# A dilated convolution on one core: two more input pairs loaded unconverted on SyncE's queue and converted by ScalarE

## The chip, the cores and the metric

The kernel runs on one core of a Trainium2 chip. The metric is the device time of one execution in microseconds (us). One execution of the kernel before was also recorded by the hardware profiler; all durations of single instructions come from that one. The engines go by the profile's names: PE (TensorE), DVE (VectorE), ACT (ScalarE), POOL (GpSimd) and SP (SyncE). All their transfers run on the core's 16 DMA engines.

## The reference

A 3x3 convolution with dilation 2 and zero padding 2, over 16 images of 64 channels, to 128 channels, in f32:

```python
batch, c_in, h, w, c_out, k, dilation = 16, 64, 64, 64, 128, 3, 2
...
x_pad = np.pad(x, ((0, 0), (0, 0), (pad, pad), (pad, pad)), mode='constant')
for b, co, ci, kh, kw in ...:
    output[b, co] += weight[co, ci, kh, kw] * x_pad[b, ci, kh*2:kh*2+h, kw*2:kw*2+w]
```

## The kernel before, in words

Two images make a pair: their 2 x 64 channels fill the 128 partitions, and each partition holds one channel's 64 x 64 values. There are eight pairs, 2 MB each in f32. Each pair's output is 4 MB in f32, two images of 128 channels.

Rows that lie two apart meet in the dilated kernel, so the kernel combines them: for each group of four rows it forms the sum of the two halves once (`s16`, by `prepare` on GpSimd, L140) and multiplies that sum by the middle row of weights; the remaining terms use differences of weights (`w21`, `w01`) and the outer rows (`w0`, `w2`), on the f16 values `x16`. The weights are turned once at the start (L98 to L127).

A pair is worked in four steps `u` of 16 rows. A step has three phases of matmuls (`phase`, L185), each for both images: the first, on `s16`, is copied by ScalarE to `s32` (L202); the other two, on `x16`, are added to `s32` by VectorE and written to the output buffer `o` (L207). SyncE stores `o` (L218): the first and the last pair in two halves, the others whole, one DMA an image.

The input gets in by two ways. Pair 0 is loaded in f32 on SyncE's queue, in two pieces, right behind the weights (L74), into one half of a buffer that otherwise holds outputs; VectorE and ScalarE convert it (L129, L131), and `prepare(0)` reads the f32 values. Pairs 1 to 7 are loaded on GpSimd's queue, which converts f32 to f16 on the way (`load`, L80). Load 1 is issued between GpSimd's two weight subtractions (L109), loads 2 to 4 after the first piece of `prepare(0)` (L146), and loads 5 to 7 from inside the loop, two pairs ahead (L194).

The order on each engine is that of the program (`manual_schedule`), and waits come from the tiles' dependencies. Buffers: six for `x16`, three for `s16`, two for `s32`, three output buffers of 4 MB (`opool`), four pairs of banks for matmul results.

Of the kernel before, what the change touches and what calls it, by code (L numbers as in the profile page):

```python
# [10 lines left out]
def kernel(  # L11
# [7 lines left out]
    nc = tc.nc  # L19

    B, CI, H, W = x.shape
# [5 lines left out]
    P = 128  # L27
    f32 = mybir.dt.float32
    f16 = mybir.dt.float16
# [20 lines left out]
    x16pool = ctx.enter_context(tc.tile_pool(name="x16pool", bufs=6))  # L50
    sumpool = ctx.enter_context(tc.tile_pool(name="sumpool", bufs=3))
    spool = ctx.enter_context(tc.tile_pool(name="spool", bufs=2))
    opool = ctx.enter_context(tc.tile_pool(name="opool", bufs=3))
# [5 lines left out]
    x_pair = x.rearrange("(nb two) c h w -> nb (two c) h w", two=2)  # L59
# [5 lines left out]
    x16 = {}  # L65
# [2 lines left out]


    cuts0 = [0, 20, 36, 52, H]  # L70
    x32 = opool.tile([P, 2, H, W], f32, tag="o", name="x32")[:, 0]
    x16[0] = x16pool.tile([P, H, W], f16, tag="x16", name="x16_0")
    for lo, hi in ((0, 36), (36, H)):
        nc.sync.dma_start(out=x32[:, lo:hi], in_=x_pair[0, :, lo:hi])  # L74


    def load(pb, cuts):
        x16[pb] = x16pool.tile([P, H, W], f16, tag="x16", name=f"x16_{pb}")
        for lo, hi in zip(cuts, cuts[1:]):
            nc.gpsimd.dma_start(out=x16[pb][:, lo:hi], in_=x_pair[pb, :, lo:hi])  # L80

    AHEAD = 5
# [16 lines left out]
    for name, a in (("w21", 2), ("w01", 0)):  # L99
        for u in range(2):  # L100
            eng = nc.vector if name == "w21" else nc.gpsimd
            eng.tensor_sub(  # L102
                out=w16[:, SLOT[name] * KW : (SLOT[name] + 1) * KW, u, :],
                in0=w32k[:, a * KW : (a + 1) * KW, :],
                in1=w32k[:, KW : 2 * KW, :],
            )

            if name == "w01" and u == 0:
                load(1, [0, H])  # L109

    w_sb = wpool.tile([P, NS * KW, CO], f16, name="w_sb")
    for n, name in enumerate(("w1", "w21", "w0", "w01", "w2")):
        ps = cpool.tile([P, 2, NB], f32, tag="ps", name=f"wt{n}")
        k0 = SLOT[name] * KW
        for j in range(KW):
            nc.tensor.matmul(  # L116
                out=ps[:, 0, j * CO : (j + 1) * CO],
                lhsT=w16[:, k0 + j, :, :].rearrange("o t i -> o (t i)"),
                rhs=ident,
                start=True,  # L120
                stop=True,
            )
        dst = w_sb[:, k0 : k0 + KW, :].rearrange("p k o -> p (k o)")
        if n % 2 == 0:
            nc.vector.tensor_copy(out=dst, in_=ps[:, 0, 0 : KW * CO])  # L125
        else:
            nc.scalar.copy(out=dst, in_=ps[:, 0, 0 : KW * CO])  # L127
        if n == 0:
            nc.vector.tensor_copy(out=x16[0][:, 0:20], in_=x32[:, 0:20])  # L129
    for lo, hi in zip(cuts0[1:], cuts0[2:]):  # L130
        nc.scalar.copy(out=x16[0][:, lo:hi], in_=x32[:, lo:hi])  # L131


    def prepare(pb, lo, hi):
        if pb not in s16:
            s16[pb] = sumpool.tile([P, 2 * NQ, W], f16, tag="s16", name=f"s16_{pb}")
        src = (x16[pb] if pb else x32).rearrange("p (q e r) w -> p q e (r w)", e=2, r=2)
        dst = s16[pb].rearrange("p (q r) w -> p q (r w)", r=2)
        q0, q1 = lo // 4, hi // 4
        nc.gpsimd.tensor_add(  # L140
            out=dst[:, q0:q1], in0=src[:, q0:q1, 0, :], in1=src[:, q0:q1, 1, :]
        )

    prepare(0, 0, 20)
    for pb in range(2, AHEAD):
        load(pb, [0, H])  # L146
    for lo, hi in zip(cuts0[1:], cuts0[2:]):
        prepare(0, lo, hi)

    def conv(pb, hb, ps, u, terms):  # L150

        p0 = hb * CI
        po = ps.rearrange("p (h w) -> p h w", w=W)
        n, total = 0, len(terms) * KW
        for name, e, shift in terms:
            for kw in KWS:
                dw = (kw - 1) * d
                lo = max(u * UR, -2 * shift)
                hi = min((u + 1) * UR, 2 * NQ - 2 * shift)
                cl, ch = max(0, -dw), min(W, W - dw)  # L160
                q0, q1 = (lo + 2 * shift) // 2, (hi + 2 * shift) // 2
                if e == 2:
                    rhs = s16[pb][p0 : p0 + CI, 2 * q0 : 2 * q1, cl + dw : ch + dw]
                else:
                    rhs = x16[pb].rearrange("p (q e r) w -> p q e r w", e=2, r=2)[
                        p0 : p0 + CI, q0:q1, e, :, cl + dw : ch + dw
                    ]
                o_ap = po[:, lo - u * UR : hi - u * UR, cl:ch]
                if e != 2:
                    o_ap = o_ap.rearrange("p (q r) w -> p q r w", r=2)  # L170
                yield dict(
                    out=o_ap,
                    lhsT=w_sb[p0 : p0 + CI, SLOT[name] * KW + kw, :],
                    rhs=rhs,
                    start=(n == 0),
                    stop=(n == total - 1),
                )
                n += 1

    def phase(pb, u, terms):  # L180

        ps = cpool.tile([CO, 2, NB], f32, tag="ps", name="ps")
        for pair in zip(*(conv(pb, hb, ps[:, hb], u, terms) for hb in range(2))):
            for m in pair:
                nc.tensor.matmul(**m)  # L185
        return ps

    for pb in range(NP):
        o = opool.tile([P, 2, H, W], f32, tag="o", name=f"o{pb}")
        ov = o.rearrange("p b (q e r) w -> p b q e (r w)", e=2, r=2)  # L190
        for u in range(NU):

            if u == 1 and AHEAD <= pb + 2 < NP:
                load(pb + 2, [0, H])  # L194
            if pb + 1 < NP:
                if u == 1:
                    prepare(pb + 1, 0, 36)
                elif u == 2:
                    prepare(pb + 1, 36, H)

            s32 = spool.tile([P, 2, NB], f32, tag="s32", name="s32")
            nc.scalar.copy(out=s32, in_=phase(pb, u, [("w1", 2, 0)]))  # L202
            for e, terms in enumerate(
                ([("w21", 1, 0), ("w0", 1, -1)], [("w01", 0, 0), ("w2", 0, 1)])
            ):
                ps = phase(pb, u, terms)
                nc.vector.tensor_add(  # L207
                    out=ov[:, :, u * UQ : (u + 1) * UQ, e, :],
                    in0=ps.rearrange("p b (q c) -> p b q c", c=QW),
                    in1=s32.rearrange("p b (q c) -> p b q c", c=QW),  # L210
                )


            step = NU // 2 if pb in (0, NP - 1) else NU
            if (u + 1) % step == 0:
                fl = slice((u + 1 - step) * 4 * UQ, (u + 1) * 4 * UQ)
                for hb in range(2):
                    nc.sync.dma_start(out=out[2 * pb + hb, :, fl], in_=o[:, hb, fl])  # L218
# [35 lines left out]
```

## Time and profile before

| | us |
|---|---|
| median of 3 runs | 127.03 |
| lowest and highest | 126.87, 127.39 |
| the profiled execution, its own time | 126.65 |
| its span | 124.9 |
| PE busy | 105.8 |
| VectorE busy | 80.8 |
| GpSimd busy | 41.5 |
| ScalarE busy | 39.6 |

The span is the time from the first to the last record of the profile; the execution's own time is 1.75 us longer. The granted TensorE clock was at 0.9 or more of full speed in every slice in which PE worked through. The page divides the span into 40 slices of 3.12 us; a digit is the busy share of a slice in tenths. A converting load is counted in the profile by the f16 bytes that it writes, 1 MB a pair, and reads twice that.

| DMA | count | KB each | median us from issue to landing |
|---|---|---|---|
| weights, SP | 1 | 288 | 2.8 |
| pair 0, SP | 2 | 1152 and 896 | 5.8 and 8.1 |
| pairs 1 to 7, POOL, converting | 7 | 1024 | 14.6 |
| stores, SP | 12 and 8 | 2048 and 1024 | 17.1 and 12.4 |

### The profile page before, as it was taken

The page shows a single profiled execution, that of the slowest core. Times are in us where ns is not written, and L with a number is a line of the kernel's source. Part 1 is how long each engine was busy: PE and PEld are TensorE (multiplying, and loading weights), DVE is VectorE, ACT ScalarE, POOL GpSimd, SP SyncE. Part 2 cuts the span into 40 slices and gives each one's busy share as a digit, 9 for nine tenths or more (in the row PEclk, how much of TensorE's full clock was granted, in tenths as well). Part 3 has the DMA queues.
Part 4 walks back from the last instruction along what each step waited for, and adds up shares of the span by engine and source line. Part 5 has one row for each costly group of instructions (what it writes and reads, how often), then busy time and mean ns, then how long its engine had stood idle before and what let it go on. Part 6 is the DMA issues. An engine that isn't in the chain of part 4 may idle for free.

```text
span 124.9 us, 2260 instructions
## 1 busy us (share of the span) xinstructions
PE 105.8 (85%) x981; PEld 56.6 (45%) x981; DVE 80.8 (65%) x71; ACT 39.6 (32%) x40; POOL 41.5 (33%) x33
## 2 busy tenths in 40 slices
PE   6359999999999999999999999999999999940000
PEld 2044555555555555555554555555555655510000
DVE  0470777787777777777739977777777777770000
ACT  4768123333333333333332333333332433300000
POOL 2879989395193019302910191000000000000000
PEclk9999999999999999999999999999999999999555
DMA  4999999999999999999999999999999999999990
GB/s 142 355 356 215 215 215 205 262 286 270 396 278 273 360 297 320 409 365 318 297 375 433 441 425 430 430 420 420 420 441 446 417 430 420 430 415 423 423 396 39
DMA packets 4329, 43.42 MB, mean 348 GB/s; under 512 B 480, under 2 KB 480, under 8 KB 736
## 3 DMA queue, kind: packets, MB, share of 16 engines
q1 hardware_dynamic: 3312, 35.95, 68.8%
q0 software_dynamic: 1008, 7.34, 28.5%
q8 instruction: 7, 0.11, 0.3%
q14 instruction: 2, 0.02, 0.0%
HBM read 17.07 MB, written 33.55 MB: 405 GB/s over the span
## 4 chain that ended last, share of the span: by engine, by line
PE 79%; DMA 5%; DVE 2%; POOL 2%; DVEq 1%; issue 0%; SPq 0%
PE ps L185 79%; DMA x<-in_x_dram 5%; DVE o L207 2%; POOL s L140 2%; DVEq L249 1%; SPq L63 0%; DVEq L207 0%
## 5 line engine op out<-in xcount | busy, mean ns | idle before, releaser
L207 DVE TENSOR_TENSOR o<-ps,s 128x1024 f32<-128x1024 f32 x64 | 76.8, 1223 | 26.4 <-PE ps L185 24.6
L185 PE MATMUL ps<-x,w_sb 64*128 64x496 f16 (+3 forms) x768 | 85.9, 369 | 0.1
L185 PEld LDWEIGHTS <-w_sb 64*128 64x128 f16 x960 | 54.3, 95 | 48.4 <-issue 3.7
L202 ACT COPY s<-ps 128x1024 f32<-128x1024 f32 x32 | 32.4, 1012 | 65.5 <-PE ps L185 65.5
L140 POOL TENSOR_TENSOR s<-x 128x1152 f16<-128x1152 f16 (+4 forms) x18 | 35.1, 1975 | 31.1 <-PE ps L185 27.7
L185 PE MATMUL ps<-s,w_sb 64*128 64x496 f16 (+1 forms) x192 | 26.6, 379 | 1.5 <-POOL s L140 1.5
L80 POOL DMA_DIRECT2D x<-in_x_dram x7 | 4.0, 579 | 0.0
L92 PE MATMUL warm<-zero 128*128 128x512 f16 x6 | 2.7, 630 | 1.2 <-DVE zero L86 1.2
L116 PE MATMUL wt<-ident,w 128*128 128x128 f16 x15 | 1.8, 312 | 2.0 <-ACT w L98 2.0
L102 DVE TENSOR_TENSOR w<-w 128x192 f16<-128x192 f32 x2 | 1.5, 799 | 2.4 <-DMA w<-in_weight_dram 2.4
L131 ACT CAST x<-x 128x1024 f16<-128x1024 f32 (+1 forms) x3 | 2.8, 974 | 0.8 <-DMA x<-in_x_dram 0.8
L116 PEld LDWEIGHTS <-w 128*128 128x128 f16 x15 | 1.5, 145 | 3.0 <-ACT w L98 3.0
L98 ACT CAST w<-w 128x576 f16<-128x576 f32 x2 | 2.3, 1220 | 1.6 <-DMA w<-in_weight_dram 1.6
L102 POOL TENSOR_TENSOR w<-w 128x192 f16<-128x192 f32 x2 | 1.9, 952 | 2.3 <-DMA w<-in_weight_dram 2.3
L125 DVE CAST w_sb<-wt 128x384 f16<-128x384 f32 x3 | 1.6, 553 | 1.4 <-PE wt L116 1.4
L92 PEld LDWEIGHTS <-zero 128*128 128x128 f16 x6 | 0.7, 137 | 2.3 <-DVE zero L86 1.2
L98 ACT ACT_TABLE_LOAD x1 | 1.3, 1283 | 0.7 <-PEq L235 0.7
L127 ACT CAST w_sb<-wt 128x384 f16<-128x384 f32 x2 | 1.0, 478 | 1.1 <-PE wt L116 1.1
L86 DVE MEMSET zero<- 128x256 uint32 x1 | 0.3, 272 | 0.9 <-PEq L235 0.9
L129 DVE CAST x<-x 128x1280 f16<-128x1280 f32 x1 | 0.8, 817 | 0.0
masks.py:199 POOL TENSOR_SCALAR_AFFINE_SELECT ident<-ident 128x128 f16<-128x128 f16 x1 | 0.3, 292 | 0.1
masks.py:197 POOL MEMSET ident<- 128x128 f16 x1 | 0.2, 204 | 0.3 <-POOLq L235 0.3
(4 smaller groups left out, 0.4 us busy)
## 6 DMA issues: line engine op xcount, KB each, us to landing
out_dram<-o SPq DMA_DIRECT2D x12, 2048.0 KB, 17.1
out_dram<-o SPq DMA_DIRECT2D x8, 1024.0 KB, 12.4
x<-in_x_dram POOLq DMA_DIRECT2D x7, 1024.0 KB, 14.6
x<-in_x_dram SPq DMA_DIRECT2D x1, 1152.0 KB, 5.8
x<-in_x_dram SPq DMA_DIRECT2D x1, 896.0 KB, 8.1
w<-in_weight_dram SPq DMA_DIRECT2D x1, 288.0 KB, 2.8
```

The costliest lines, as they stand in the source:

```text
L80: nc.gpsimd.dma_start(out=x16[pb][:, lo:hi], in_=x_pair[pb, :, lo:hi])
L92: nc.tensor.matmul(out=warm[:, 0], lhsT=zero[:, 0:P], rhs=zero, start=True, stop=True)
L98: nc.scalar.copy(out=w16[:, 0:NK, u, :], in_=w32k)
L102: eng.tensor_sub(out=w16[:, SLOT[name] * KW : (SLOT[name] + 1) * KW, u, :], in0=w32k[:, a * KW : (a + 1) * KW, :], in1=w32k[:, KW : 2 * KW ...
L116: nc.tensor.matmul(out=ps[:, 0, j * CO : (j + 1) * CO], lhsT=w16[:, k0 + j, :, :].rearrange("o t i -> o (t i)"), rhs=ident, start=True, st ...
L125: nc.vector.tensor_copy(out=dst, in_=ps[:, 0, 0 : KW * CO])
L131: nc.scalar.copy(out=x16[0][:, lo:hi], in_=x32[:, lo:hi])
L140: nc.gpsimd.tensor_add(out=dst[:, q0:q1], in0=src[:, q0:q1, 0, :], in1=src[:, q0:q1, 1, :])
L185: nc.tensor.matmul(**m)
L202: nc.scalar.copy(out=s32, in_=phase(pb, u, [("w1", 2, 0)]))
L207: nc.vector.tensor_add(out=ov[:, :, u * UQ : (u + 1) * UQ, e, :], in0=ps.rearrange("p b (q c) -> p b q c", c=QW), in1=s32.rearrange("p b ( ...
L249: with _tile.TileContext(nc) as tc:
```

## The change

Pairs 1 and 2 are now loaded like pair 0: in f32, on SyncE's queue, each as one DMA, issued right behind pair 0's two pieces. Pair 1 takes the other half of the output buffer that pair 0 stands in, pair 2 half of the next one. So output 0 takes the third buffer, output 1 the first, output 2 the second. ScalarE converts each of the two pairs in three pieces (rows 0 to 16, 16 to 32, 32 to 64), one behind its copy to `s32` in steps 1, 2 and 3 of the pair before. `prepare` reads the f32 values for pairs 0 to 2. GpSimd's load 1 and load 2 are gone; its loads 3 and 4 are issued after the whole of `prepare(0)`. Loads 5 to 7 stay where they are. No matmul, add or store changes.

```diff
-    x32 = opool.tile([P, 2, H, W], f32, tag="o", name="x32")[:, 0]
-    x16[0] = x16pool.tile([P, H, W], f16, tag="x16", name="x16_0")
-    for lo, hi in ((0, 36), (36, H)):
-        nc.sync.dma_start(out=x32[:, lo:hi], in_=x_pair[0, :, lo:hi])
+    PLAIN = 3
+    x32 = []
+    for pb in range(PLAIN):
+        if pb % 2 == 0:
+            stage = opool.tile([P, 2, H, W], f32, tag="o", name=f"x32_{pb}")
+        x32.append(stage[:, pb % 2])
+        x16[pb] = x16pool.tile([P, H, W], f16, tag="x16", name=f"x16_{pb}")
+        for lo, hi in ((0, 36), (36, H)) if pb == 0 else ((0, H),):
+            nc.sync.dma_start(out=x32[pb][:, lo:hi], in_=x_pair[pb, :, lo:hi])
+
+    def cast(eng, pb, lo, hi):
+        eng(out=x16[pb][:, lo:hi], in_=x32[pb][:, lo:hi])
...
-            if name == "w01" and u == 0:
-                load(1, [0, H])
...
-        src = (x16[pb] if pb else x32).rearrange("p (q e r) w -> p q e (r w)", e=2, r=2)
+        src = (x32[pb] if pb < PLAIN else x16[pb]).rearrange("p (q e r) w -> p q e (r w)", e=2, r=2)
...
     prepare(0, 0, 20)
-    for pb in range(2, AHEAD):
-        load(pb, [0, H])
     for lo, hi in zip(cuts0[1:], cuts0[2:]):
         prepare(0, lo, hi)
+
+    for pb in range(PLAIN, AHEAD):
+        load(pb, [0, H])
...
             nc.scalar.copy(out=s32, in_=phase(pb, u, [("w1", 2, 0)]))
+            if pb + 1 < PLAIN and u:
+                lo, hi = ((0, 16), (16, 32), (32, H))[u - 1]
+                cast(nc.scalar.copy, pb + 1, lo, hi)
```

More of the change, by code (lines that the diff above doesn't have):

```diff
@@ L128 @@
         if n == 0:
-            nc.vector.tensor_copy(out=x16[0][:, 0:20], in_=x32[:, 0:20])
+            cast(nc.vector.tensor_copy, 0, 0, 20)
     for lo, hi in zip(cuts0[1:], cuts0[2:]):
-        nc.scalar.copy(out=x16[0][:, lo:hi], in_=x32[:, lo:hi])
+        cast(nc.scalar.copy, 0, lo, hi)
     def prepare(pb, lo, hi):
```

## The prediction

> **What bounds the kernel now.** I read the page first, for the share of busy time along the span; then the windows, for the transfer rate stage by stage; then the chain of waits; then the waits of each engine.
>
> ```profile
> PE   6359999999999999999999999999999999940000
> DMA  4999999999999999999999999999999999999990
> q1 hardware_dynamic: 3312, 35.95, 68.8%
> q0 software_dynamic: 1008, 7.34, 28.5%
> ```
>
> PE works without a break from slice 3 and stops in slice 35. The 16 DMA engines are full from slice 1 to slice 38, four slices longer. The queues' shares add up to 97.3% of the span: SyncE's queue (q1) moved the weights, pair 0 and all stores, GpSimd's (q0) the seven converting loads. Those count 7.34 MB as written in f16, and read twice that in f32.
>
> ```profile
> 109.61 1.23 DVE o L207
> 110.83 1.13 DVEq L249
> ```
>
> The chain of waits ends in the last add, at 110.84 us. The 14 us after it belong to no compute engine. What runs there is seen in the windows (columns: window, length, busy us of each engine, granted clock, DMA share, GB/s):
>
> ```profile
> 0.00:2.00 2.00, 0.81 (x2) 0.28 (x3) 0.27 (x1) 1.26 (x1) 0.70 (x6) 1.00 0.15 21
> 2.00:3.50 1.50, 1.50 (x5) 0.45 (x3) 0.00 (x0) 0.02 (x1) 0.00 (x0) 1.00 1.03 335
> 3.50:5.00 1.50, 0.43 (x2) 0.00 (x0) 1.41 (x2) 1.42 (x2) 1.36 (x2) 1.00 0.99 350
> 5.00:8.00 3.00, 1.78 (x15) 1.61 (x16) 1.58 (x4) 1.93 (x4) 2.20 (x3) 1.00 0.98 408
> 9.00:18.00 9.00, 8.75 (x66) 4.32 (x67) 4.05 (x4) 3.70 (x4) 9.00 (x9) 1.00 1.03 215
> 21.00:22.50 1.50, 1.50 (x18) 0.79 (x16) 0.99 (x1) 1.01 (x1) 1.50 (x2) 1.00 1.07 169
> 80.00:110.00 30.00, 30.00 (x294) 16.52 (x292) 23.05 (x20) 10.12 (x10) 0.00 (x0) 1.00 1.01 427
> 110.00:120.00 10.00, 0.61 (x8) 0.18 (x4) 1.96 (x2) 0.00 (x0) 0.00 (x0) 0.78 1.00 425
> ```
>
> After PE stops, stores drain at 425 GB/s, the rate they had beside PE (427). From 9 to 18 us only converting loads move: 215 GB/s written is 430 GB/s read. Counted by the f32 side, every stage after 5 us is thus near 410 to 430 GB/s with a DMA share near 1.0, whatever the mix. The end is set by the sum of transfers, 50.6 MB (16.8 of x, 0.3 of weights, 33.55 of output), begun at about 2 us. 50.6 / 0.427 = 118.5 us; the slow windows before 5 us, the dip at 21 us and the end of the last store account for the rest of the 124.9.
>
> ```profile
> SPq L218 <- DVE o L207: 100.1, 10, 16.8
> POOL s L140 <- PE ps L185: 27.7, 4, 8.4
> ACT s L202 <- PE ps L185: 65.5, 31, 2.6
> ```
>
> SyncE waits for results and never for room, and GpSimd and ScalarE wait mostly for PE: the compute engines have slack, and DMA has none.
>
> **How much slack.** The last four stores (1 MB each) need 4.2 MB / 0.427 = 9.8 us, the last two 4.9 us. Those two are issued from 112.0 us. The queue is still full to about 123.5 us, so their data need come to the front only at 118.6; allowing 2 to 3 us for a DMA to start, PE may be 3 to 4 us late before the end moves.
>
> **The change, part by part.**
>
> *Bytes.* Pairs 1 and 2 are read in f32 in both kernels. On the f32 side nothing is added or removed.
>
> *Rate of the two loads.* This is the only term on the path. Converting: 4.194 MB / 0.430 = 9.75 us for the two. A plain 2 MB load alone in steady state is not in the trace, so I bound it. By the queues' shares: q0 took 0.285 x 124.9 / 7 = 5.09 us a load; q1 took 0.688 x 124.9 = 85.9 us for 35.95 MB, or 5.01 us for 2.097 MB; two loads gain 0.15 us. By the stores' windows (427 GB/s): 9.82 us, 0.07 us lost. By pair 0's own load, the only plain load of x: 350 and 408 GB/s in 3.5 to 8 us, mean 389, so 10.78 us, 1.03 us lost; by its later part alone (408), 0.53 us lost. I take 0.0, between the first two, because stores have the same queue and the same 16 KB per partition as the new loads, while pair 0 runs in the start-up, where the rate still climbs from 335. Both ends, -0.15 and +1.03, stay for the range.
>
> *Order at the start.* Today GpSimd issues load 1 at 4.69 us, loads 2 to 4 from 9.14. Afterwards SyncE issues pairs 1 and 2 right behind pair 0, at about 2.1 to 2.9 us (two issues of 0.42 us each). The engines were full from 2 us anyway, so starting earlier fills no hole: 0 us. Before 2 us the weights are on their way in both kernels. SyncE's stores come behind the new loads in its queue: the first is issued at 18.85 us, when pair 2 is through at about 8.3 + 9.8 = 18.1 (19.1 at 389 GB/s), so they lose at most 0.3 us of waiting, while the engines stay full.
>
> *Does a hole open before load 3?* Loads 3 and 4 now stand behind the whole of prepare(0) on GpSimd: its first piece ends at 9.21, then 1.29 + 1.29 + 1.01 us give 12.8, then two issues of at most 0.70 us. The quickest converting load landed 9.2 us after its issue, 4.3 more than its transfer takes. Even with all of that as latency, load 3's data start at 12.8 + 0.6 + 4.3 = 17.7, before 18.1. So 0, with 0.4 us to spare by that bound; one us of hole would cost one us.
>
> *GpSimd's sums from f32.* Its f32 pieces cost 2.5 to 2.6 ns an element (1292 ns for 512, 1013 for 384; 3.5 for the first, 2217 for 640); its f16 ones 2.05 (2367 for 1152). A pair of 2048 elements goes from 4.25 to 5.2 to 7.1 us, so 1 to 2.9 us more for each of two pairs. prepare(1) then runs from about 14.1 to 19.3 or 21.2, prepare(2) to 24.5 or 28.3; PE needs their sums from about 21.9 and 34.5 (9.25 plus 12.65 a pair). prepare(3) waited for its load until 25.16 before; now it ends by 30 to 32.5, and load 5, behind it, is issued there instead of at 29.3. By then 15.0 MB are queued, enough to about 37 us. Cost 0; the cover is that queue.
>
> *ScalarE.* Pieces of 1024 elements took 1.05 us, so a pair costs 1.05 + 1.05 + 2.1 = 4.2 us, two pairs 8.4. A copy (1.01) plus a piece is 2.06 us, or 3.1 with the large one, in a period of 101 / 32 = 3.16 us. What queues behind a piece is the next copy to s32, for which VectorE's adds wait; PE reads pair 1's f16 behind the last piece. The last copy of pair 0 starts at 21.44, so that piece ends at about 24.55, when PE turns to pair 1's first x16 phase. Delay of PE between 0 and perhaps 0.5 us a pair, inside its 3 to 4 us. If that cover were gone, it would be 1 us.
>
> *Output buffers.* x32_0 and x32_1 share one, x32_2 takes the next. o1 waits for the last read of pair 1 (24.55 us) and is first written at about 25; o2 comes a pair later. From o3 on every output waits for the store of the output three before, as now. Cost 0.
>
> **Sum.** 0.0 (bounds -0.15 and +1.03) + 0 + 0 + 0: 126.65 us on the profiled execution. The median of three runs, 127.03, is 0.38 above that execution; the forecast on that scale is 127.0.
>
> **Rivals.**
>
> *Slower: plain loads run at pair 0's rate.* For it: the only plain load rows, 350 and 408 GB/s against 430 for converting loads. Against: the rate climbs through that load, and the stores of the same queue hold 427. Price 1.03 us, time 128.1; it decides below 404 GB/s (4.194 / 0.404 = 9.75 + 0.63). Chance 0.13. The Trainium skill's "DMA: Bandwidth & Descriptors" (Where 436 GB/s comes from) has a nearby rule: transfers between HBM and SBUF are held by the HBM side at about 358 GB/s. By that the two plain loads would take 11.7 us, an estimate from that page of 2 us lost; this trace disagrees, with 430 read and 427 written, except in the windows before 5 us.
>
> *Slower: the hole before load 3.* If GpSimd reaches load 3 over 1 us later than reckoned (first piece at 3.5 ns an element for all: 512 + 512 + 384 would add 1.3 us), DMA idles from 18.1 to about 19.0: 127.9. Against: engines at 1.03 share now, and the 4.3 us are mostly queueing. Chance 0.03.
>
> *Faster: converting loads hold DMA up in ways beyond their own time.* The dip at 21 to 22.5 us (169 instead of 215) lost 0.32 us while they ran. If it goes with two of them on the other queue, and the share's 0.15 us comes too, 126.55. To pass 0.5% it takes 0.64 us, and a plain rate above 460 GB/s; no row is that high. Chance 0.12 that something of this kind passes the bound.
>
> *The change does nothing to the bound* is the forecast itself, 0.72.
>
> **How the numbers follow.** About 0.5% (0.64 us) is what a measurement of this kernel can tell from no change: the three runs alone span 0.52. No change 0.72 (126.4 to 127.7); slower 0.13 + 0.03 = 0.16; faster 0.12. The forecast's own cases lie within 126.5 to 127.6. The range goes from 126.3 to 127.9: downward a little past the faster rival, upward to the hole's price and most of the plain rate's.
>
> **What would show it.** Right: DMA full from slice 1 to 38 with GB/s near 427 where 215 stood from 9 to 18 us; the last add again near 111 us and the stores draining behind it; q0 down to five loads at 5.09 us; ScalarE about 8.4 us busier. Wrong: a rate under 404 GB/s between 9 and 18 us, a slice of less than 9 tenths near 18 us, a first store much after 19 us, or PE's last matmul beyond 114 us.

## The result and the profile after

| | us, median | against before | ratio, 95% interval |
|---|---|---|---|
| changed kernel | 133.94 | 127.0 | 1.0531 [1.0508, 1.0555] |

The change made the kernel 5.3% slower, where no change was forecast. Ratios compare undisturbed executions only, so they need not be the quotient of two medians. The profiled execution took 133.38 us, with a span of 131.6, 6.7 more than before. The page, as before (busy share in 40 slices of 3.29 us, then the two queues):

```profile
PE   6359999999997029999999999999999999994000
DMA  5999999999999999957999999999959957999993
q1 hardware_dynamic: 3600, 40.14, 73.7%
q0 software_dynamic: 720, 5.24, 19.6%
```

Two things are new. PE has a hole in slices 12 to 14, and DMA, full throughout before, has thin places in slices 17, 18 and 29 to 33. The queues' shares add up to 93.3% of a longer span. The chain of waits (start, length, what) shows the hole:

```profile
26.07 0.33 SPq L227
26.40 0.04 issue
26.44 11.97 DMA out_dram<-o
38.41 8.89 issue
47.30 0.05 DVEq L216
47.35 0.04 issue
47.39 1.24 DVE o L216
48.63 0.04 issue
48.67 70.29 PE ps L191 x660
...
120.28 1.13 DVEq L258
```

VectorE's previous add ends at 38.41 us, and its next one, at L216, starts only at 47.39. The chain leads to the stores of `o` that SyncE issued from 26.07 us on, output 0's second half. From 38.41 on the profile gives the wait to "issue", that is, to nothing it can see. But the last of these stores was issued at 26.44 us and took 20.8 us to land, so it landed at 47.2, just before the add. The first step of pair 2 is where this add stands; the 660 matmuls behind it are the rest of the kernel. The waits by pairs (total, times, longest) show who stood behind it:

```profile
ACT s L208 <- DVE o L216: 10.9, 1, 10.9
DVE o L216 <- issue: 9.0, 1, 9.0
PE ps L191 <- DVE o L216: 6.7, 1, 6.7
```

PE stood still for 6.7 us, yet the last add ended 9.4 us later than before (120.29 against 110.84). The rest is PE's own work, 108.5 us busy against 105.8. Most of it stands right behind the hole, where the granted clock was 0.50: in the same 4 us the profile has 20 matmuls instead of 43 (the first line is the changed kernel, the second the kernel before):

```profile
48.60:52.60 4.00, 3.93 (x20) 1.66 (x21) 3.48 (x4) 0.00 (x0) 0.00 (x0) 0.50 1.01 313
48.60:52.60 4.00, 4.00 (x43) 2.14 (x41) 3.51 (x4) 1.40 (x2) 2.38 (x3) 1.00 1.01 375
```

The four windows below (columns as before) show the new loads, and where DMA lost its time:

```profile
9.00:16.00 7.00, 6.64 (x38) 2.94 (x39) 1.86 (x2) 2.69 (x3) 6.67 (x7) 1.00 0.99 426
56.00:60.00 4.00, 4.00 (x45) 2.15 (x40) 2.82 (x3) 1.94 (x2) 4.00 (x2) 1.00 0.41 172
90.00:100.00 10.00, 10.00 (x100) 5.26 (x98) 7.53 (x7) 3.84 (x4) 0.00 (x0) 1.00 0.86 361
100.00:112.00 12.00, 12.00 (x120) 6.23 (x116) 9.64 (x8) 3.68 (x5) 0.00 (x0) 1.00 0.83 351
```

The plain loads run at 426 GB/s. Later the DMA engines run dry: the share falls 2.4, 1.4 and 2.0 us short of full in these windows, 5.8 of the 6.7 us. Pair 2's results come 9 us late, so output 1's stores are nearly through when output 2's are issued, at 59.6 us. DMA is full again from 60 to 90 us and runs short once more after that, and the chain runs through PE for its last 70 us: PE, not DMA, sets the pace.

Why does output 2 wait for output 0? The waits that the built programs carry tell it; the runs have no print of them, but they show the wait itself, and the experiments move it. Before, output 2's first add waits for pair 0's load, conversion and sums (it takes the staging buffer), and output 3's for output 0's stores. In the changed program output 2's first add waits for the four stores of output 0, and output 3's for pair 2's load and sums. The buffers go round in the order in which their last users stand in the program. Pair 2's staging buffer has its last user in pair 1's step 3, behind output 0's last store, so output 0's buffer is free first on paper and goes to output 2, although on the chip its stores land much later than pair 2 is converted.

### The profile page after: what moved, and what is told of

It is laid out like the page before. It is cut to its first block, busy times and chain, and to the rows that moved or that the text cites. A ratio compares the mean times of both kernels' runs of the same rounds, so it can differ in the third digit from the quotient of the medians.

```text
span 131.6 us, 2267 instructions
## 1 busy us (share of the span) xinstructions
PE 108.5 (82%) x981; PEld 55.1 (42%) x981; DVE 80.8 (61%) x71; ACT 47.0 (36%) x46; POOL 41.5 (32%) x31
## 4 chain that ended last, share of the span: by engine, by line
PE 66%; DMA 14%; issue 7%; DVE 2%; POOL 2%; DVEq 1%; SPq 1%
PE ps L191 66%; DMA out_dram<-o 9%; DMA x<-in_x_dram 4%; DVE o L216 2%; POOL s L145 2%; DVEq L258 1%; SPq L63 0%; SPq L227 0%; DVEq L216 0%
## 5 line engine op out<-in xcount | busy, mean ns | idle before, releaser
L216 DVE TENSOR_TENSOR o<-ps,s 128x1024 f32<-128x1024 f32 x64 | 76.7, 1223 | 35.9 <-PE ps L191 23.7
L191 PE MATMUL ps<-x,w_sb 64*128 64x496 f16 (+3 forms) x768 | 87.9, 376 | 6.7 <-DVE o L216 6.7
L191 PEld LDWEIGHTS <-w_sb 64*128 64x128 f16 x960 | 52.9, 96 | 59.3 <-issue 13.9
L145 POOL TENSOR_TENSOR s<-x 128x1152 f16<-128x1152 f16 (+6 forms) x18 | 36.0, 2021 | 40.5 <-PE ps L191 28.5
L191 PE MATMUL ps<-s,w_sb 64*128 64x496 f16 (+1 forms) x192 | 27.1, 386 | 1.6 <-POOL s L145 1.6
L82 ACT CAST x<-x 128x1024 f16<-128x1024 f32 (+2 forms) x9 | 10.8, 1213 | 0.4 <-DMA x<-in_x_dram 0.4
L88 POOL DMA_DIRECT2D x<-in_x_dram x5 | 2.9, 589 | 0.0
```

Of the source, the lines that this page charges most:

```text
L82: eng(out=x16[pb][:, lo:hi], in_=x32[pb][:, lo:hi])
L145: nc.gpsimd.tensor_add(out=dst[:, q0:q1], in0=src[:, q0:q1, 0, :], in1=src[:, q0:q1, 1, :])
L216: nc.vector.tensor_add(out=ov[:, :, u * UQ : (u + 1) * UQ, e, :], in0=ps.rearrange("p b (q c) -> p b q c", c=QW), in1=s32.rearrange("p b ( ...
```

## The experiments

The theory: the loss is output 2's wait for output 0's stores, with what follows from it, and nothing else that the change does. The rival: the loss is the new work, ScalarE's conversions, GpSimd's f32 sums, the two loads on SyncE's queue.

**The changed kernel with the buffers in another order.** One instruction is added, with the one-element tile that it writes and a name for output 0:

```diff
+    mark = wpool.tile([P, 1], f32, name="mark")
...
+        o_first = o if pb == 0 else o_first
...
                 cast(nc.scalar.copy, pb + 1, lo, hi)
+                if pb == 1 and u == 3:
+                    nc.scalar.copy(out=mark, in_=o_first[:, 0, 0, 0:1])
```

> The changed kernel with one more instruction: ScalarE reads one element of output 0 behind the last piece of pair 2's conversion, so that output 0's buffer has its last user after pair 2's staging buffer, and output 2 is put in the staging buffer instead of output 0's. All loads, conversions and sums stay as changed. Theory (the loss is output 2's wait for output 0's stores): the 9 us idle of VectorE at 38 us is gone, PE ends near 111 us, time 127.0, between 126.5 and 127.6. Rival (the loss is the new work on ScalarE, GpSimd and SyncE's queue, and the stall only shows it): 133 to 134, as the changed kernel.

Measured 127.11 against 126.89, ratio 1.0015 [0.9998, 1.0032]. Its chain runs through PE without a break:

```profile
9.32 100.37 PE ps L192 x948
...
111.00 1.13 DVEq L262
```

By its profile VectorE has no wait for a store at all, the add that ends the chain ends at 111.0, and DMA is full to slice 37. All of the change's loads, conversions and sums are in this kernel. The rival falls.

**The kernel before with that buffer order alone.** No load or conversion is moved:

```diff
+    held = opool.tile([P, 2, H, W], f32, tag="o", name="held")
+    mark = wpool.tile([P, 1], f32, name="mark")
+    nc.vector.memset(held[:, 0, 0, 0:1], 0.0)
...
             nc.scalar.copy(out=s32, in_=phase(pb, u, [("w1", 2, 0)]))
+            if pb == 1 and u == 3:
+                nc.scalar.copy(out=mark, in_=held[:, 0, 0, 0:1])
```

> The kernel before, all loads and conversions as they were, with one output buffer kept from the start until pair 1's last step by a one-element write and a one-element read, so that output 2 takes output 0's buffer. Theory: VectorE waits for output 0's stores at about 38 us for 8 to 10 us, 133 to 134.5. Rival (the new work): 127.0, since none of it is here.

Measured 134.87 against 126.89, ratio 1.0613 [1.0566, 1.0660]: the whole loss, and more, without the change's work. Here the profile names the wait (waits, then the chain):

```profile
DVE o L213 <- DMA out_dram<-o: 12.4, 1, 12.4
PE ps L189 <- DVE o L213: 10.1, 1, 10.1
```

```profile
25.40 24.27 DMA out_dram<-o
...
122.60 1.13 DVEq L255
```

Output 0's last stores are issued at 25.0 to 25.4 us and land by 49.67, 2.5 us later than in the changed kernel, and the wait is longer, 12.4 instead of 9.0 us.

**One pair at a time.** In the first kernel, against the changed one:

```diff
-    PLAIN = 3
+    PLAIN = 2
```

In the second, pair 2 takes the free half of pair 0's staging buffer, and load 1 goes back to GpSimd:

```diff
-    PLAIN = 3
+    PLAIN = (0, 2)
...
-        if pb % 2 == 0:
+        if pb == 0:
...
-        x32.append(stage[:, pb % 2])
+        x32[pb] = stage[:, pb // 2]
...
+            if name == "w01" and u == 0:
+                load(1, [0, H])
...
-        src = (x32[pb] if pb < PLAIN else x16[pb]).rearrange("p (q e r) w -> p q e (r w)", e=2, r=2)
+        src = (x32[pb] if pb in PLAIN else x16[pb]).rearrange("p (q e r) w -> p q e (r w)", e=2, r=2)
...
-    for pb in range(PLAIN, AHEAD):
+    for pb in range(3, AHEAD):
...
-            if pb + 1 < PLAIN and u:
+            if pb + 1 in PLAIN and u:
```

> Pair 1 alone is loaded unconverted, into the free half of pair 0's staging buffer; pair 2 stays a converting load. No second output buffer is taken, and output 2 takes the staging buffer. Theory: 127.0, between 126.5 and 127.6. Rival (cost in proportion to the moved work): half the loss, about 130.4.

> Pair 2 alone is loaded unconverted, into the free half of pair 0's staging buffer; pair 1 stays a converting load. That buffer is now read until pair 1's last step, so output 2 is put in output 0's buffer, with half of the moved work. Theory: the full stall, 133 to 134.5. Rival (cost in proportion to the moved work): about 130.4.

Pair 2 alone: 130.14 against 126.89, ratio 1.0274 [1.0227, 1.0322]. That is the rival's number, not the theory's. The profile shows the theory's wait, but a shorter one (waits, then the chain):

```profile
DVE o L219 <- DMA out_dram<-o: 6.0, 1, 6.0
```

```profile
26.45 17.83 DMA out_dram<-o
...
117.01 1.13 DVEq L261
```

That the rival's number came out is chance: the first experiment has all of the moved work and loses nothing. My 133 to 134.5 took the landing time for fixed. It is not: the wait for the store ends at 44.28 here, at 47.30 in the changed kernel, at 49.67 with the held buffer. The spans are 127.9, 131.6 and 133.6, so 83.6, 84.3 and 83.9 us behind the landing. The time left then is nearly the same, and the cost follows the time of the landing.

Pair 1 alone: 128.10, ratio 1.0095 [1.0075, 1.0115]. Half the rival's size and outside the theory's range: something else costs 1.2 us. Output 2 takes the staging buffer here, so it isn't that wait. The windows behind pair 1's load (GB/s last):

```profile
13.00:14.00 1.00, 1.00 (x8) 0.38 (x6) 0.43 (x1) 0.00 (x0) 1.00 (x3) 0.50 1.30 115
14.00:15.00 1.00, 1.00 (x10) 0.51 (x8) 0.37 (x1) 0.00 (x0) 0.99 (x2) 0.77 0.39 49
15.00:16.00 1.00, 1.00 (x14) 0.53 (x10) 0.86 (x1) 0.73 (x1) 1.00 (x1) 1.00 0.63 131
```

Converting loads alone moved 215 GB/s before. Pair 1's load, issued at 2.1 us, has landed 11.8 us later, at 13.9, and load 2, issued by GpSimd at 12.34, isn't up to speed before 16. The three windows fall short of 215 GB/s by what takes 1.6 us to move.

Two other things in this profile could be blamed. PE's granted clock is 0.50 in the first of these windows; but the six runs of this kernel, with mean clocks from 0.934 to 0.957, all lie between 127.92 and 128.31 us, and the first experiment's profile, with 0.64 from 9 to 16 us, took 126.89. And VectorE waits 4.0 us for a store before pair 4's first add (output 4 waits for output 1's); but the last add ends at 112.68, 1.8 us later than before, less than the 3 to 4 us by which PE was reckoned to be free to run late. The second of the next two runs settles it.

**Two more runs follow from these.** One moves output 0's landing in the changed kernel and leaves its buffers alone; the other closes the hole of pair 1 alone.

```diff
-            if u == 1 and AHEAD <= pb + 2 < NP:
+            if u == (3 if pb == 3 else 1) and AHEAD <= pb + 2 < NP:
```

> The changed kernel, with output 2 still in output 0's buffer, but load 5 issued behind prepare(4), at about 39 us instead of 30.3, so that output 0's stores share the DMA engines with one load less. Theory (the loss is the time at which output 0's last store lands; in the three kernels with that wait the span was 83.6, 84.3 and 83.9 us more than that time): it lands at 42 to 43 us instead of 47.3, the span is 126 to 127, the time 127.7 to 129. Rival (the loss is in the buffer's reuse as such, or in the wait's place, whatever lies in the queues): 133 to 134.

Measured 127.8 against 126.98, ratio 1.0046 [1.0009, 1.0083]. Output 2 still has output 0's buffer, since loads take nothing from that pool, but nothing is left of the wait: pair 2's first add starts at 40.57 us after 0.91 us of idle (0.60 in the kernel before), and PE works without a break (timeline, then the chain):

```profile
40.57 2.35 DVE L216 TENSOR_TENSOR o<-ps,s 128x1024 f32<-128x1024 f32 x2 [0.91 <-PE ps L191]
```

```profile
10.89 100.54 PE ps L191 x948
```

Its profiled execution took 130.13 us, with pair 0 landing 1.5 us later than in the others, so I read little else from it. The time came out at the low end of what was expected, and the stores landed before 40.57, earlier than the 42 to 43 expected. About 6 of the 6.9 us are gone by moving a load that output 2's buffer does not depend on. So the wait's price is set by when the stores land, and that by what shares the DMA engines with them. It keeps a loss of 0.5%. A hole in DMA stands where load 5 used to be:

```profile
38.00:39.00 1.00, 1.00 (x13) 0.53 (x11) 1.00 (x2) 0.82 (x1) 1.00 (x2) 1.00 0.40 164
39.00:40.00 1.00, 1.00 (x14) 0.63 (x12) 0.66 (x1) 0.97 (x1) 1.00 (x1) 1.00 0.14 57
40.00:41.00 1.00, 1.00 (x14) 0.48 (x10) 0.43 (x1) 0.04 (x1) 1.00 (x3) 1.00 0.62 262
```

That this hole is the 0.5% is an argument, not shown.

For the other, pair 1 alone, loads 2 to 4 are issued behind the first piece of `prepare(0)`:

```diff
     prepare(0, 0, 20)
+    for pb in range(PLAIN, AHEAD):
+        load(pb, [0, H])
     for lo, hi in zip(cuts0[1:], cuts0[2:]):
         prepare(0, lo, hi)
-
-    for pb in range(PLAIN, AHEAD):
-        load(pb, [0, H])
```

> Pair 1 alone loaded unconverted, as in pair1_only, but loads 2 to 4 issued behind the first piece of prepare(0), at about 9 us as in the kernel before, instead of at 12.3 us. Theory (pair1_only's 1.2 us are a hole in the DMA engines from 13 to 15.5 us, between pair 1's last byte and load 2's first): the hole is gone, 127.0, between 126.5 and 127.5. Rival (the plain load or ScalarE's and GpSimd's new work costs it): 128.1, as pair1_only.

Measured 126.96 against 126.98, ratio 0.9999 [0.9967, 1.0032], and the same three windows are full:

```profile
13.00:14.00 1.00, 1.00 (x14) 0.50 (x10) 1.00 (x1) 0.00 (x0) 1.00 (x2) 1.00 1.15 246
14.00:15.00 1.00, 1.00 (x13) 0.48 (x11) 1.00 (x2) 0.23 (x1) 0.39 (x1) 1.00 0.94 197
15.00:16.00 1.00, 1.00 (x12) 0.53 (x10) 0.36 (x1) 1.00 (x2) 0.71 (x1) 1.00 0.98 205
```

VectorE still waits 2.6 us for the store before pair 4, and it costs nothing here. The 1.2 us were the late issue of GpSimd's loads, not the plain load. No version beat the kernel before by more than its interval: two of them reach the sum of the transfers, which the change doesn't touch.

## Why the prediction was wrong

*What failed: "Output buffers", "Cost 0".* The text ahead of the prediction gave output 2 the second buffer, pair 2's staging buffer. The prediction said that output 1 takes the first staging buffer, "o2 comes a pair later", and that "from o3 on every output waits for the store of the output three before, as now". It took the buffers to go round by number. They go round by their last users' place in the program: output 2 waits for the output two before, and the staging buffer goes to output 3. Priced at 0, it cost VectorE 9.0 us of wait, PE 6.7 us of standing and 2.7 us of slower work behind it, and the span 6.7 us. Of the rivals none had it. One of the listed signs did: PE's last matmul beyond 114 us (it ended at about 119). The signs near 18 us did not show.

*How much slack: right, if a little high.* The prediction gave PE 3 to 4 us before the end moves. The last add ended 9.4, 11.8 and 6.2 us later than before's 110.84 (changed kernel, held buffer, pair 2 alone), the spans grew by 6.7, 8.7 and 3.0: the difference is 2.7 to 3.2 us.

*Rate of the plain loads: right.* 426 GB/s in 9 to 16 us, against the 404 below which it would have decided; with the wait gone the whole change is worth 1.0015. The first of the slower rivals is out, and so is the rule that stood beside it, of the Trainium skill's "DMA: Bandwidth & Descriptors" (Where 436 GB/s comes from): 358 GB/s for transfers between HBM and SBUF does not bind here.

*The hole before load 3: right that it is covered.* In the changed kernel the DMA share is 1.00 from 9 to 18 us and 1.03 from 18 to 21. Pair 2's data came later than the 18.1 us reckoned: GpSimd waited for them until 21.50, as load 3 moved beside them (273 GB/s from 18 to 21 us, between 427 for plain and 215 for converting transfers), and this too stayed hidden. With pair 1 alone there is a hole, and some 1.6 us of missing transfer cost 1.2 us; the prediction had reckoned one us for one.

*GpSimd and ScalarE: right in sign and cover, too high in size.* Groups of the changed kernel:

```profile
L145 POOL TENSOR_TENSOR s<-x 128x1152 f16<-128x1152 f32 x2 | 5.2, 2624 | 2.9 <-DMA x<-in_x_dram 2.9
L145 POOL TENSOR_TENSOR s<-x 128x896 f16<-128x896 f32 x2 | 4.2, 2094 | 0.0
L82 ACT CAST x<-x 128x2048 f16<-128x2048 f32 x2 | 3.8, 1902 | 0.0
```

A pair's sums from f32 take 4.7 us, 0.5 more than from f16, not 1 to 2.9; ScalarE became 7.4 us busier, not 8.4. A piece of 2048 takes 1.90 and not 2.1, which makes the two pairs 8.0; and the profile has each of the six pieces begin about 0.1 us before the copy ahead of it ends. Both stayed hidden.

*The faster rival* found nothing: the change's version without the wait is not faster than before.

## What to carry to other kernels

A tile that borrows a slot from a pool of output buffers changes who waits for whom long after it is gone; before pricing such a change, read off the built program which earlier user each later tile waits for, and when that user's last transfer lands. A kernel bound by transfers can look safe against anything on its engines, but its stores land late, here up to 26.5 us behind their issue; a buffer handed back by a store turned that lateness into an engine's stall. The amount of slack read from the tail of the profile held to within 1 us, and it tells how much of such a stall reaches the end.

## What the hardware showed that I had not expected

Where the other queue had run empty, GpSimd's converting load took from its issue at 12.34 us to about 16 us to reach full rate, 3.7 us in which the windows fell to 115, 49 and 131 GB/s; issued at about 9 us, with other data still flowing, it cost nothing. PE's hole had a second price: behind it the granted clock was 0.50 until 52.6 us, and PE was busy 2.7 us longer with the same work; the held buffer's profile has 0.52 from 50 to 55 us in the same place. And in the changed kernel the profile books the wait that the whole loss hangs on, 9.0 us, as "issue", while it books the same wait under the store's name in two of the experiments: a long "issue" on an engine that should have been ready was a transfer.
